# A hybrid layer on one core: two sums moved by one step, a second buffer for a sum of tokens, and the last norm ahead of a split

## The chip, the cores and the metric

The kernel runs on one core of a Trainium2 chip. The core has five engines that run side by side: TensorE (PE in the profile, with its weight loads as PEld), VectorE (DVE), ScalarE (ACT), GpSimd (POOL) and SyncE (SP), which here only issues DMAs. Each engine works through its own list of instructions in order and waits at semaphores for the others. The metric is the device time of one execution in microseconds, lower is better.

## What is computed

One layer of a backbone over 1024 latent tokens and 256 context tokens with 1024 features: a normalised and modulated input goes through one input projection, then an mLSTM head group and a windowed attention head group, an output projection with a residual, and a gated convolutional feed-forward block with a second residual and a last norm. The change lies where attention ends and the feed-forward begins, so these lines matter:

```python
y_a = window_attention(...)
x = x + g_a * (jnp.concatenate([y_m, y_a], axis=-1) @ w_out[l])
x = x + g_f * conv_glu(modulate(rmsnorm(x, norm_ffn[l]), sh_f, sc_f),
                       w_up[l], ffn_conv_w[l], ffn_conv_b[l], w_down[l])

def conv_glu(h, w_up, conv_w, conv_b, w_down):
    a, val = jnp.split(h @ w_up, 2, axis=-1)
    a = jax.nn.gelu(dwconv(a, conv_w, conv_b))
    return (a * val) @ w_down
```

## The kernel before

All products are float32-accurate on a faster format: each operand is split into a high part (a cast, mostly on ScalarE) and a low part (source minus high part, on VectorE), and three matmuls per product are added up. The names end in `h` and `l`. The cast and the subtraction of a split are issued separately, so a split is two places in the code: `split_b(b)` and its kin issue the cast at once and return a function that issues the subtraction.

**Attention** runs over 32 pairs of heads, block by block of 128 tokens, in a software pipeline of steps `t` from 0 to n + 1 with n = 32. In one step different stages serve different pairs: scores of pair t + 1, normalisation of the pair before (`nrm`, GpSimd), transposition to `pt` and split into `ph` and `pl` (L1166, L1172), the product with the values into `u` (L1182), and the two copies and two adds that write `u` into `yT` (L1187 to L1194). There is a single `u` buffer, so the product of one pair waits for the adds of the pair before. Other work is put in at numbered places of a step: `more[t, i]` is a list that `fill(t, i)` issues at place i of step t. Place 3 is ahead of the splits of its step on VectorE. Steps 32 and 33 are the last: there is no new score and few pairs are still in the pipeline.

**The weight sums.** The feed-forward's first matrix is multiplied in a scheme with fewer products than the plain one, in which the operands are sums of quarters: seven operands of tokens (`B11`, `B21`, `B22`, `T1` to `T4`, all in the two tiles `hB`, high and low) and sums of weight quarters. For block 0 of the weights the quarters lie in `ym` during attention, and three operations on VectorE at `more[n, 3]` (step 32) write the sums into `yS`, a view of `yT`. When all readers of `ym` are done, its room is taken by `er`, `e0` and `r1`, into which `load_0` loads quarters again (L1261, issued by SyncE).

**The second residual's input.** After attention a loop goes over the blocks in `order = [4, 1, 5, 2, 6, 3, 7]`. Each takes the output projection of a block (`wout_n`, two halves), adds the residual (L1388), squares it on ScalarE (`sq`), takes the root and its reciprocal (`norm_b`), transposes (`trans`) and moves the result to `raws` (`evac`). From pairs of blocks b - 4 and b, four sums follow: `sum1` to `sum4` on VectorE, and the splits `split_t1` to `split_t4` into `hB`. `sum2` writes to a tile `tb` with one buffer, which `sum4` and `split_t2` read. The projection's input is a split of `yT` into `yh`, `yl` (`ysplit_h`, `ysplit_l`); the first three blocks of the order have buffers of their own, the later four lie in slots of `hB` that are not needed yet.

**The end of that loop.** The last block is 7, `prev` is 3 and `late` is 6. Its norm is the head of a chain: square, root, reciprocal, scaling in two halves (ScalarE and VectorE), transposes, the splits for T1 to T4 of blocks 6 and 7. TensorE meanwhile computes what needs neither (`ps_a`, `ps_a2`), and then the products of block 0: `f` (B22), `c` (T1), `b` (T2), `e` (T3), `d` (T4), and goes on with block 1.

The order of work on TensorE, VectorE, ScalarE and GpSimd is that of the code, written by hand. The order of SyncE's DMAs around the change is chosen by the planner, from L1643 on also by the code.

Of the kernel before, what the change touches and what calls it, by code (L numbers as in the profile page):

```python
# [9 lines left out]
F32 = mybir.dt.float32  # L10
F32R = mybir.dt.float32r
# [7 lines left out]
P = 128  # L19
# [59 lines left out]
def build(tc, I, out, dbg=None):  # L79
    nc = tc.nc  # L80
    dbg = dbg or {}
    V, S, G, T = nc.vector, nc.scalar, nc.gpsimd, nc.tensor
# [41 lines left out]
    ym = rp.tile([P, NL, 512], F32, name="ym")  # L124
# [5 lines left out]
    hl = [hl_(0)]  # L130
# [13 lines left out]
    def load_split(src, w, rawf=None, split=True, alloc=True, now=range(2)):  # L144
        room = lambda: [st.tile([P, KT, XW], F32R, name=n, tag=n)[:].rearrange("p a b -> p (a b)")[:, :KT * w]
                        .rearrange("p (k f) -> p k f", k=KT) for n in ("wh", "wl")]
        hi, lo = room() if alloc else (None, None)
        raws = {}

        def load(q):  # L150
            raws[q] = rawf() if rawf else sr.tile([P, 4, XW], F32, name="wr", tag="wr")
            nc.sync.dma_start(raws[q][:, :, :w], src[:, 4 * q:4 * q + 4, :])

        def cut(q):
            ks, raw = slice(4 * q, 4 * q + 4), raws[q]
            S.copy(hi[:, ks, :w], raw[:, :, :w])
            V.tensor_tensor(out=lo[:, ks, :w], in0=raw[:, :, :w], in1=hi[:, ks, :w].bitcast(F32), op=ALU.subtract)

        if split:
            for q in range(2):  # L160
                load(q)
                cut(q)
            return hi, lo
        for q in now:
            load(q)

        def rest(qs=range(2)):
            nonlocal hi, lo
            if hi is None:
                hi, lo = room()  # L170
            for q in qs:
                cut(q)
            return hi, lo
        rest.load = load
        return rest
# [296 lines left out]
    order = (list(range(NCH)), [1, 0] + list(range(NCH - 1, NC - 1, -1)))  # L472
# [491 lines left out]
    n = 0  # L964
# [12 lines left out]
    for h in range(H):  # L977
# [3 lines left out]
        else:  # L981
            wq = [wkq]
            late = lambda: wq.append(load_split(I["w_q"][1], 256, lambda: pq.tile([P, 4, 256], F32, name="wr", tag="rga")))
# [66 lines left out]
    yslice = lambda b: next(v[:, t.index(b)] for t, v in yTa.items() if b in t)  # L1050
# [3 lines left out]
    t4 = pb_.enter_context(tc.tile_pool(name="t4", bufs=2, reuse_waits="tile"))  # L1054
# [7 lines left out]
    class Wout:  # L1062
# [32 lines left out]
        def add(self, n):  # L1095
            ns = slice(512 * n, 512 * n + 512)
            V.tensor_tensor(out=self.xb[:, ns], in0=self.po[:], in1=self.xb[:, ns], op=ALU.add)
            if n == 1:
                nc.sync.dma_start(x2_d[self.b][:], self.xb[:])
# [96 lines left out]
    order = [4, 1, 5, 2, 6, 3, 7]  # L1196
    ys = {}
    sub = lambda e, o, x, y: e.tensor_tensor(out=o, in0=x, in1=y, op=ALU.subtract)  # L1198

    def ysplit_h(b, eng=G, room=None):  # L1200
        ys[b] = room or [t4.tile([P, 4, P], F32R, name=f"y{n}", tag=f"y{n}", bufs=3)[:] for n in "hl"]
        eng.copy(ys[b][0], yslice(b)) if eng is S else eng.tensor_copy(ys[b][0], yslice(b))

    def ysplit_l(b):
        sub(V, ys[b][1], yslice(b), ys[b][0].bitcast(F32))
# [13 lines left out]
    more = collections.defaultdict(list)  # L1219
# [28 lines left out]
    n = len(pairs)  # L1248
# [4 lines left out]
    more[n - 5, 2] += [lambda: ysplit_l(order[0])]  # L1253
    more[n - 4, 0] += [lambda: ysplit_h(order[1], S)]
    more[n - 3, 0] += [lambda: ysplit_l(order[1])]
    more[n - 2, 0] += [lambda: ysplit_h(order[2], S)]
    add = lambda e, o, x, y: e.tensor_tensor(out=o, in0=x, in1=y, op=ALU.add)
    yS = yTa[2, 0, 4, 1, 5][:].rearrange("p w k t -> p w (k t)")

    def load_0(to, h):  # L1260
        nc.sync.dma_start(to, I["w_up"][0, :, 2 * h:2 * h + 2].rearrange("p q k f -> p q (k f)"))  # L1261

    more[n - 11, 0] += [lambda: load_0(ym[:, 2:4], 0), lambda: load_0(ym[:, 4:6], 1)]
    more[n, 3] += [lambda: add(V, yS[:, 2], ym[:, 5], ym[:, 4]), lambda: sub(V, yS[:, 3], yS[:, 2], ym[:, 2]),
                   lambda: sub(V, yS[:, 1], ym[:, 3], yS[:, 3])]

    attn = tc.manual_schedule(engines={mybir.EngineType.PE, mybir.EngineType.DVE, mybir.EngineType.Activation,
                                       mybir.EngineType.Pool})
# [4 lines left out]
    for t in range(n + 2):  # L1273
# [3 lines left out]
        if t in WOT:  # L1277
            k = 4 + WOT.index(t)
            room = [wop.tile([P, D], F32R, name=f"wo{n}{k}")[:] for n in "hl"]
# [70 lines left out]
    hB = [hbp.tile([P, 7, 4, 512], F32R, name=f"hB{i}") for i in range(2)]  # L1350
    tbk = ExitStack()
    tbp = tbk.enter_context(tc.tile_pool(name="tbp", bufs=1, side="right", reuse_waits="tile"))
    B11, B21, B22, T1, T2, T3, T4 = range(7)
# [19 lines left out]
    hns, rs, pts, raws, tbs = ({} for _ in range(5))  # L1373
    last = order[-1]
# [15 lines left out]
    def mean0(b):  # L1390
        V.tensor_scalar(out=rs[b][:, 2:3], in0=rs[b][:, 0:1], scalar1=1.0 / D, scalar2=EPS, op0=ALU.mult, op1=ALU.add)

    def sq(b, n, mean=True):
        if n == 0:
            hns[b] = t5.tile([P, D], F32, name="hn", tag="hn")
            rs[b] = t5.tile([P, 3], F32, name="r2", tag="r2")
        ns = slice(512 * n, 512 * n + 512)
        S.activation(hns[b][:, ns], xs[b][:, ns], AF.Square, accum_out=rs[b][:, n:n + 1])
        if n == 1:
            if mean:  # L1400
                run(1)
                mean0(b)
            S.activation(rs[b][:, 0:1], rs[b][:, 1:2], AF.Sqrt, bias=rs[b][:, 2:3], scale=1.0 / D)

    def norm_b(b, halves=False):
        run(1)
        V.reciprocal(rs[b][:, 0:1], rs[b][:, 0:1])
        if halves:
            S.activation(hns[b][:, 0:512], xs[b][:, 0:512], AF.Copy, scale=rs[b][:, 0:1])
            V.tensor_scalar(out=hns[b][:, 512:D], in0=xs[b][:, 512:D], scalar1=rs[b][:, 0:1], scalar2=None, op0=ALU.mult)  # L1410
        else:
            S.activation(hns[b][:], xs[b], AF.Copy, scale=rs[b][:, 0:1])
# [28 lines left out]
    def run(n=99):  # L1441
        for _ in range(min(n, len(held))):
            held.pop(0)()

    def split(b, blk, w, src, hi_eng=S):
        ts = slice(b % 4 * P, b % 4 * P + P)
        hi, lo = (hB[i][:, blk:blk + w, :, ts] for i in range(2))
        (S.copy if hi_eng is S else hi_eng.tensor_copy)(hi, src)  # L1448
        return lambda: sub(V, lo, src, hi.bitcast(F32))


    def sum1(b):
        sub(V, raws[b - 4][:, 0], raws[b][:, 0], raws[b - 4][:, 0])

    def sum2(b):
        tbs[b] = tbp.tile([P, 1, 4, P], F32, name="tb", tag="tb", bufs=1)
        sub(V, tbs[b][:, 0], raws[b][:, 1], raws[b - 4][:, 0])

    def sum3(b, e=V):
        sub(e, raws[b][:, 0], raws[b][:, 1], raws[b][:, 0])  # L1460

    def sum4(b, e=V):
        sub(e, raws[b - 4][:, 1], raws[b - 4][:, 1], tbs[b][:, 0])

    split_b = lambda b: split(b, B22, 1, raws[b][:, 1:2])
    split_t1 = lambda b: split(b, T1, 1, raws[b - 4][:, 0:1])
    split_t2 = lambda b: split(b, T2, 1, tbs[b][:])
    split_t3 = lambda b: split(b, T3, 1, raws[b][:, 0:1])
    split_t4 = lambda b: split(b, T4, 1, raws[b - 4][:, 1:2])
# [10 lines left out]
    add = lambda e, o, x, y: e.tensor_tensor(out=o, in0=x, in1=y, op=ALU.add)  # L1480
# [3 lines left out]
    fence.__enter__()  # L1484
    sq(0, 0)
    sq(0, 1)
    for j in range(3, 7):
        ysplit_h(order[j], G, [hB[n][:, B22 + j - 3, :, 3 * P:4 * P] for n in range(2)])
    for j in range(2, 5):
# [3 lines left out]
    late = None  # L1493
    for i, b in enumerate(order):
# [20 lines left out]
        if pp is not None and pp < 4:  # L1515
# [4 lines left out]
            late = None  # L1520
            run(1)
        if pp is not None and pp >= 4:
# [6 lines left out]
            late = pp  # L1529
# [11 lines left out]
    evac(prev)  # L1541
    add1()
    late = pp
    lo_b = split_b(late)
    mean0(last)
    lo3 = split(prev, B11, 2, raws[prev][:], V)
    sq(last, 1, False)
    sum1(late)
    norm_b(last, True)
    lo3()  # L1550
    prod(ps_a, e0, 0, B11, True, True, None, c3)
    prod(ps_a2, e0, 1, B21, True, False, None, c3, range(2))
# [14 lines left out]
    f = ExitStack()  # L1567
# [20 lines left out]
    def wsplit_h(R, n):  # L1588
        src = (R[0] and R[0][:], R[1][:, 2:4], R[1][:, 0:2] if R[0] else r1[:], R[1][:, 4:5] if R[0] else yS[:, 1:2])[n]
        w = src.shape[1]  # L1590
        wt = [fw.tile([P, w, 512], F32R, name=f"w{n}{w}", tag=f"w{n}{w}", bufs=5 if w == 2 else 2) for n in "hl"]
        S.copy(wt[0][:], src)  # L1592

        def lo():
            sub(V, wt[1][:], src, wt[0][:].bitcast(F32))
            return wt
        return lo
# [5 lines left out]
    lo_b = split_b(last)  # L1603
# [9 lines left out]
    lo_2 = split_t2(late)  # L1613
    wS = wS()
    S.copy(ar0[:], ps_a[:])
    lo_1()
    lo_2()
    sum3(late)
    sum4(late)
    sum2(last)  # L1620
    lo_3, lo_4 = split_t3(late), split_t4(late)
    lo_2 = split_t2(last)
    wA = wsplit_h(R, 2)
    lo_2()
    sum3(last)
    lo_5 = split_t3(last)
    lo_3()
# [8 lines left out]
                                                                    tag={"a": "a", "f": "b", "b": "b"}.get(n, "c"))  # L1636
# [118 lines left out]
    for i in range(1, NF):  # L1755
        last = i == NF - 1
# [175 lines left out]
    more = {}  # L1932
# [87 lines left out]
    for t, (p, ps, fresh) in enumerate(products):  # L2020
        for j in range(NP):
            n = NP * t + j
# [34 lines left out]
            if NP + 3 <= n < NP + 3 + NL:  # L2057
                b = n - NP - 3
# [17 lines left out]
    n = len(steps) - 3  # L2076
# [100 lines left out]
```

## Time and profile before

| what | value |
|---|---|
| median of 3 runs | 1268.82 us (1268.67 to 1268.99) |
| profiled execution | 1268.82 us |
| its span | 1267.0 us |
| mean granted TensorE clock | 0.998 |
| instructions in the span | 19250 |

A row of the timeline has: start in us from the span's start, duration in us, engine, line, operation, output and input, shape, how many instructions were merged, and in brackets the engine's idle time before it in us with what ended it. A row of the table by stretches has the stretch, its length, then the busy time and number of instructions of PE, PEld, DVE, ACT and POOL, the granted clock, the busy share of the DMA engines and GB/s. Matmul ends are modelled, so the start of a matmul is firmer than its end.

### The profile page before, as it was taken

The page shows a single profiled execution, that of the slowest core. Times are in us where ns is not written, and L with a number is a line of the kernel's source. Part 1 is how long each engine was busy: PE and PEld are TensorE (multiplying, and loading weights), DVE is VectorE, ACT ScalarE, POOL GpSimd, SP SyncE. Part 2 cuts the span into 40 slices and gives each one's busy share as a digit, 9 for nine tenths or more (in the row PEclk, how much of TensorE's full clock was granted, in tenths as well). Part 3 has the DMA queues.
Part 4 walks back from the last instruction along what each step waited for, and adds up shares of the span by engine and source line. Part 5 has one row for each costly group of instructions (what it writes and reads, how often), then busy time and mean ns, then how long its engine had stood idle before and what let it go on. Part 6 is the DMA issues. An engine that isn't in the chain of part 4 may idle for free.

```text
span 1267.0 us, 19250 instructions
## 1 busy us (share of the span) xinstructions
PE 1234.5 (97%) x7047; PEld 1059.8 (84%) x7047; DVE 974.1 (77%) x1691; ACT 639.0 (50%) x1309; POOL 187.7 (15%) x162
## 2 busy tenths in 40 slices
PE   6999999999999999999999999999999999999997
PEld 4799999999898888887877888888888887788886
DVE  5863777777887888788987877777777776877887
ACT  6632556464865777786843333333333334434435
POOL 1200000000001434221002231233231232001000
PEclk9999999999999999999999999999999999999999
DMA  9541535362255333104313332223322237975553
GB/s 360 184 142 35 144 119 152 116 180 70 85 175 162 130 129 105 59 27 167 116 51 125 111 106 100 94 106 117 101 107 100 92 134 267 337 251 187 194 193 133
DMA packets 90560, 176.17 MB, mean 139 GB/s; under 512 B 12954, under 2 KB 29538, under 8 KB 90466
## 3 DMA queue, kind: packets, MB, share of 16 engines
q1 hardware_dynamic: 90178, 174.15, 40.9%
q8 instruction: 56, 0.92, 0.3%
q10 hardware_dynamic: 288, 0.79, 0.2%
q14 instruction: 38, 0.31, 0.1%
HBM read 136.58 MB, written 38.33 MB: 138 GB/s over the span
## 4 chain that ended last, share of the span: by engine, by line
PE 80%; DVE 7%; ACT 5%; DMA 4%; issue 2%; SPq 1%; POOL 1%; ACTq 0%; DVEq 0%; POOLq 0%
PE pd L2014 14%; PE pa L1476 8%; PE pc L1476 8%; PE pp L588 7%; PE pe L1476 4%; PE pd L1476 4%; PE pb L1476 4%; PE u L1182 3%; PE pv L307 2%; PE pv L309 2%; PE pv L308 2%; PE pt L1159 2%; PE po L307 1%; PE px L309 1%; PE po L309 1%
## 5 line engine op out<-in xcount | busy, mean ns | idle before, releaser
L1592 ACT CAST wh<-Rb 128x1024 fp32r<-128x1024 f32 (+1 forms) x63 | 57.0, 906 | 144.3 <-PE pd L1476 77.2
L2014 PE MATMUL pd<-dh,al 128*128 128x512 f32 x296 | 115.4, 390 | 1.2 <-DVE al L1357 1.2
L2014 PE MATMUL pd<-dh,ah 128*128 128x512 f32 x296 | 115.3, 389 | 0.0
L2014 PE MATMUL pd<-dl,ah 128*128 128x512 f32 x296 | 115.3, 389 | 0.0
L1476 PE MATMUL pc<-hB,wh 128*128 128x512 f32 x344 | 105.6, 389 | 0.0
L1476 PE MATMUL pa<-hB,wh 128*128 128x512 f32 x336 | 103.7, 390 | 0.3 <-ACT sn L1673 0.2
L1198 DVE TENSOR_TENSOR wl<-Rb,wh 128x1024 fp32r<-128x1024 f32 (+1 forms) x63 | 65.8, 1046 | 39.3 <-ACT wh L1592 38.7
L1709 POOL TENSOR_TENSOR tt<-vt,tt 128x512 f32<-128x512 f32 x22 | 29.5, 1342 | 369.0 <-ACT tt L1703 369.0
L588 PE MATMUL pp<-hl,wh 128*128 128x512 f32 x256 | 79.3, 405 | 0.0
L307 PE MATMUL pv<-wh,hl 128*128 128x256 f32 x256 | 75.9, 296 | 0.0
L1476 PEld LDWEIGHTS pc<-hB,wh 128*128 128x128 f32 x344 | 64.6, 188 | 13.5
L1476 PEld LDWEIGHTS pa<-hB,wh 128*128 128x128 f32 x336 | 62.9, 188 | 14.2 <-ACT sn L1673 1.1
L309 PE MATMUL pv<-wh,hl 128*128 128x256 f32 x256 | 72.4, 283 | 0.0
L308 PE MATMUL pv<-wl,hl 128*128 128x256 f32 x256 | 72.3, 282 | 0.0
L2014 PEld LDWEIGHTS pd<-dh,al 128*128 128x128 f32 x296 | 55.6, 188 | 13.2 <-DVE al L1357 1.9
L1476 PE MATMUL pc<-hB,wl 128*128 128x512 f32 x172 | 66.4, 389 | 0.0
L2014 PEld LDWEIGHTS pd<-dl,ah 128*128 128x128 f32 x296 | 55.6, 188 | 11.9 <-DVE dl L1357 0.3
L2014 PEld LDWEIGHTS pd<-dh,ah 128*128 128x128 f32 x296 | 55.6, 188 | 11.8 <-ACT ah L1356 0.3
L1476 PE MATMUL pa<-hB,wl 128*128 128x512 f32 x168 | 65.4, 389 | 0.0
L1166 ACT CAST ph<-pt 128x512 fp32r<-128x512 f32 (+1 forms) x88 | 46.2, 525 | 26.8 <-PE pt L1159 26.5
L1476 PE MATMUL pb<-hB,wh 128*128 128x512 f32 x176 | 54.0, 390 | 0.6 <-ACT hB L1448 0.6
L1136 DVE TENSOR_REDUCE nm<-sps 128x1 f32<-128x641 f32 (+1 forms) x64 | 50.3, 786 | 4.9 <-PE sps L1132 3.4
(1080 smaller groups left out, 3698.9 us busy)
## 6 DMA issues: line engine op xcount, KB each, us to landing
w<-in_w_ada_dram SPq DMA_DIRECT2D x64, 256.0 KB, 2.7
br<-in_w_down_dram SPq DMA_DIRECT2D x25, 512.0 KB, 5.6
ar<-act_s SPq DMA_DIRECT2D x44, 256.0 KB, 3.5
Ra<-in_w_up_dram SPq DMA_DIRECT2D x21, 512.0 KB, 3.6
Rb<-in_w_up_dram SPq DMA_DIRECT2D x21, 512.0 KB, 3.6
act_a<-tt SPq DMA_DIRECT2D x33, 256.0 KB, 2.0
act_s<-tt SPq DMA_DIRECT2D x33, 256.0 KB, 2.0
wr<-in_w_h_dram SPq DMA_DIRECT2D x16, 512.0 KB, 4.0
```

The costliest lines, as they stand in the source:

```text
L307: T.matmul(ps, st_hi, mv_hi, start=first, stop=False)
L308: T.matmul(ps, st_hi, mv_lo, start=False, stop=False)
L309: T.matmul(ps, st_lo, mv_hi, start=False, stop=last)
L588: T.matmul(pp[:, 512 * n:512 * n + 512], wkq[sw][:, kt, cs], hl[n][part][:, kt, :], start=kt == 0 and sw + part == 0, stop=kt == KT - 1 an ...
L1136: V.tensor_reduce(out=self.nm[:, j:j + 1], in_=self.sv[j], axis=AX.X, op=ALU.max, negate=True)
L1166: S.copy(self.ph[i][:, :w], self.pt[i][:, :w])
L1182: T.matmul(self.u[:], vv[:, c, self.g], part[i][:, kk * 2 * P:(kk + 1) * 2 * P], start=kb + m == 0, stop=kb == last and m == 1)
L1198: sub = lambda e, o, x, y: e.tensor_tensor(out=o, in0=x, in1=y, op=ALU.subtract)
L1476: T.matmul(ps[:, cols], wt[sw][:, j, kt * P:kt * P + P], hB[part][:, blk, kt, cols], start=first and n == 0, stop=last and n == len(seq) - ...
L1592: S.copy(wt[0][:], src)
L1709: G.tensor_tensor(out=self.tt[:, h2_], in0=self.vt[:], in1=self.tt[:, h2_], op=ALU.mult)
L2014: T.matmul(ps[:], ac[sa][:, js], w[sw], start=first and n == 0, stop=last and n == 2, skip_group_check=not fresh)
```

## The change

Three parts, which a fourth makes room for.

First, of the three sums of block 0's weights only the first stays in step 32; the second and third go to the same place of step 33. Second, after the loop, the split of block 6 for B22 (`lo_b = split_b(late)`, whose cast is on ScalarE) is issued behind the norm of block 7 instead of ahead of its square. Third, `tb` has two buffers, and `sum2(last)` with the split for T2 goes ahead of `sum3(late)` and `sum4(late)`. For the room, `yl` has two buffers instead of three, and the low part of the third block of the order (block 5) lies in the slot of `hB` that T4 of block 7 takes later.

```diff
     def ysplit_h(b, eng=G, room=None):
-        ys[b] = room or [t4.tile([P, 4, P], F32R, name=f"y{n}", tag=f"y{n}", bufs=3)[:] for n in "hl"]
+        room = room or [None, None]
+        ys[b] = [a if a is not None else t4.tile([P, 4, P], F32R, name=f"y{n}", tag=f"y{n}", bufs=3 if n == "h" else 2)[:]
+                 for a, n in zip(room, "hl")]
...
-    more[n - 2, 0] += [lambda: ysplit_h(order[2], S)]
+    yh2 = []
+    more[n - 2, 0] += [lambda: yh2.append(t4.tile([P, 4, P], F32R, name="yh", tag="yh", bufs=3)[:]),
+                       lambda: S.copy(yh2[0], yslice(order[2]))]
...
-    more[n, 3] += [lambda: add(V, yS[:, 2], ym[:, 5], ym[:, 4]), lambda: sub(V, yS[:, 3], yS[:, 2], ym[:, 2]),
-                   lambda: sub(V, yS[:, 1], ym[:, 3], yS[:, 3])]
+    more[n, 3] += [lambda: add(V, yS[:, 2], ym[:, 5], ym[:, 4])]
+    more[n + 1, 3] += [lambda: sub(V, yS[:, 3], yS[:, 2], ym[:, 2]), lambda: sub(V, yS[:, 1], ym[:, 3], yS[:, 3])]
...
-        tbs[b] = tbp.tile([P, 1, 4, P], F32, name="tb", tag="tb", bufs=1)
+        tbs[b] = tbp.tile([P, 1, 4, P], F32, name="tb", tag="tb", bufs=2)
...
+    ys[order[2]] = [yh2[0], hB[1][:, T4, :, 3 * P:4 * P]]
     for j in range(3, 7):
...
     late = pp
-    lo_b = split_b(late)
     mean0(last)
     lo3 = split(prev, B11, 2, raws[prev][:], V)
     sq(last, 1, False)
     sum1(late)
     norm_b(last, True)
+    lo_b = split_b(late)
     lo3()
...
     lo_1()
+    sum2(last)
     lo_2()
+    lo_2 = split_t2(last)
     sum3(late)
-    sum4(late)
-    sum2(last)
-    lo_3, lo_4 = split_t3(late), split_t4(late)
-    lo_2 = split_t2(last)
+    lo_3 = split_t3(late)
     wA = wsplit_h(R, 2)
     lo_2()
+    sum4(late)
+    lo_4 = split_t4(late)
     sum3(last)
```

## The prediction

> **What bounds the kernel now.** I read the page's busy table first, then the busy time by stretches, then TensorE's timeline with the idle time before each row.
>
> ```profile
> PE 1234.5 (97%) x7047; PEld 1059.8 (84%) x7047; DVE 974.1 (77%) x1691; ACT 639.0 (50%) x1309; POOL 187.7 (15%) x162
> ```
> ```profile
> 585.00:622.00 37.00, 37.00 (x188) 31.07 (x187) 35.03 (x76) 28.87 (x66) 0.00 (x0) 1.00 0.53 185
> ...
> 700.00:1000.00 300.00, 300.00 (x1325) 248.40 (x1324) 231.16 (x256) 102.87 (x112) 75.92 (x48) 1.00 0.30 105
> ```
> ```profile
> 572.66 0.47 PE L1182 MATMUL u<-ph,vv 128*128 128x256 f32 x2 [1.58 <-DVE yT L1194]
> ...
> 627.11 0.65 PE L1424 MATMUL pt<-ident,hn 128*128 128x128 f32 x4 [0.49 <-DVE hn L1410]
> ...
> 638.05 1.20 PE L1476 MATMUL pb<-hB,wh 128*128 128x512 f32 x4 [0.63 <-ACT hB L1448]
> ...
> 650.07 0.50 PE L1476 MATMUL pb<-hB,wl 128*128 128x512 f32 x1 [0.30 <-DVE wl L1198]
> ```
>
> The first row says TensorE is the resource: 1234.5 of 1267.0 us. The stretches (TensorE is the second figure) say it never rests from 585 to 622 or from 700 to 1000. So an edit to VectorE or ScalarE pays only if it shortens one of TensorE's few pauses, and what it wins there lasts, because behind the pause TensorE alone sets the pace. The four timeline rows are the pauses beside the change: one per part of it, and the last just downstream. Together they hold 3.0 us; no more can be won than about that and the slow restart after each.
>
> **Part A: two of block 0's sums go from step 32 to step 33.**
>
> ```profile
> 568.53 0.67 DVE L1257 TENSOR_TENSOR yT<-ym 128x512 f32<-128x512 f32 x1
> 569.24 1.07 DVE L1198 TENSOR_TENSOR yT<-yT,ym 128x512 f32<-128x512 f32 x1
> 570.34 1.07 DVE L1198 TENSOR_TENSOR yT<-ym,yT 128x512 f32<-128x512 f32 x1
> 571.33 0.68 DVE L1172 TENSOR_TENSOR pl__7377<-pt,ph 128x512 fp32r<-128x512 f32 x1
> 571.93 0.27 DVE L1193 TENSOR_TENSOR yT<-u,ut 64x128 f32<-64x128 f32 x1
> 572.22 0.29 DVE L1194 TENSOR_TENSOR yT<-u,ut 64x128 f32<-64x128 f32 x1
> ...
> 575.48 0.69 DVE L1172 TENSOR_TENSOR pl__7416<-pt,ph 128x512 fp32r<-128x512 f32 x1 [1.65 <-ACT ph L1166]
> ...
> 583.72 0.68 DVE L1510 CAST e0h<-er 128x1024 fp32r<-128x1024 f32 x1
> ```
> ```profile
> 569.28 0.59 ACT L1166 CAST ph<-pt 128x512 fp32r<-128x512 f32 x1 [0.86 <-PE pt L1159]
> ...
> 574.86 0.59 ACT L1166 CAST ph<-pt 128x512 fp32r<-128x512 f32 x1 [3.81 <-PE pt L1159]
> ```
> ```profile
> 570.68 0.40 PE L309 MATMUL po<-woh,yml 128*128 128x512 f32 x1
> ...
> 578.12 0.40 PE L1182 MATMUL u<-pl__7416,vv 128*128 128x256 f32 x2
> ```
>
> The three sums hold VectorE until 571.41. Behind them wait the split `pl__7377` and the two adds of L1193 and L1194, and these empty the one `u` buffer that TensorE wants at 572.66. Take the last two sums away: the split's other input is ScalarE's `ph`, done at 569.28 + 0.59 = 569.87, so it starts at 569.90 (0.03 for the hand-over, as from 574.86 + 0.59 to 575.48). The adds end 572.51 - 571.33 = 1.18 after the split's start, so at 571.08, and TensorE follows 0.15 later as now (572.66 - 572.51), at 571.23, with its own earlier work done at 571.08. The start moves by 572.66 - 571.23 = **1.43 us**. What is late next is the same chain, by 0.15 us.
>
> The sums now stand ahead of the split `pl__7416` on VectorE. There it idled 1.65 us for ScalarE; two sums at 0.69 take 1.4, at today's 1.07 they take 2.2 and push the split by 0.5. Its reader is the `u` matmul at 578.12, 1.95 after the split's end (576.17), so I cost them at nothing either way; without that slack they would cost up to 0.5. Why were they 1.07 long?
>
> ```profile
> 554.36 0.70 POOL L1147 TENSOR_SCALAR p__7138<-p__7138,ss 128x512 f32<-128x512 f32 x1
> ...
> 568.78 0.99 POOL L1147 TENSOR_SCALAR p__7322<-p__7322,ss 128x512 f32<-128x512 f32 x1 [3.14 <-DVE ss L1144]
> ```
> ```profile
> 554.45 0.69 DVE L1172 TENSOR_TENSOR pl__7182<-pt,ph 128x512 fp32r<-128x512 f32 x1 [0.36 <-ACT ph L1166]
> ```
>
> GpSimd ran beside them and was itself slow (0.99 against 0.70). The split `pl__7182` ran beside GpSimd at its plain 0.69, so I leave the advanced split at 0.69. The lower bound, had it 1.07, is 1.43 - 0.39 = 1.04 us. [...]
>
> The two loads into `er` and `r` are issued when the old `ym` is free, so they move with the last sum.
>
> ```profile
> 571.49 0.33 SPq L1261 DMA_DIRECT2D er<-in_w_up_dram  x1
> ...
> 584.30 0.33 SPq L1378 DMA_DIRECT2D x<-x_d  x1
> ```
> ```profile
> er<-in_w_up_dram SPq DMA_DIRECT2D x1, 512.0 KB, 4.0
> ```
>
> The sums end near 573.8, the load lands at 573.8 + 0.1 + 4.0 = 577.9, and the first reader is the cast of L1510 at 583.72 - 1.43 = 582.3: 4.4 us of cover. The low part of block 5's `y` in a free slot of `hB` has the same operation, type and length as in its old buffer: nothing.
>
> **Part B: the norm of block 7 ahead of a split on ScalarE.**
>
> ```profile
> 624.73 0.65 ACT L1448 CAST hB<-raw 128x512 fp32r<-128x512 f32 x1
> 625.25 0.67 ACT L1398 ACTIVATE hn<-x 128x512 f32<-128x512 f32 x1
> ...
> 626.04 0.29 ACT L1403 ACTIVATE r<-r 128x1 f32<-128x1 f32 x1
> ```
> ```profile
> 624.09 0.69 DVE L1388 TENSOR_TENSOR x<-po,x 128x512 f32<-128x512 f32 x1
> ...
> 625.52 0.68 DVE L1198 TENSOR_TENSOR raw<-raw 128x512 f32<-128x512 f32 x1
> 626.37 0.16 DVE L1407 RECIPROCAL r<-r 128x1 f32<-128x1 f32 x1 [0.17 <-ACT r L1403]
> 626.57 0.49 DVE L1410 TENSOR_SCALAR hn<-x,r 128x512 f32<-128x512 f32 x1
> ```
>
> Without the cast in front, the square starts when its input is added, 624.09 + 0.69 + 0.03 = 624.81 instead of 625.25: 0.44 earlier, the root then ends at 625.89. But the reciprocal stands behind the sum of 625.52 on VectorE, and unhindered operations of this kind start 0.60 apart (571.33 to 571.93). So it starts at 626.12, not 626.37: the gain is **0.25**, not 0.44, and VectorE's sum is late next. TensorE still pauses about 0.24 there. The cast now runs behind ScalarE's half of the norm, until about 627.6, still ahead of its reader. Bounds: 0.1, if the casts behind it slip, to 0.44.
>
> **Part C: the sum for T2 ahead of sums 3 and 4, with a second `tb` buffer.**
>
> ```profile
> 635.92 0.69 DVE L1198 TENSOR_TENSOR raw<-raw,tb 128x512 f32<-128x512 f32 x1
> 636.65 0.69 DVE L1198 TENSOR_TENSOR tb<-er,raw 128x512 f32<-128x512 f32 x1
> 638.03 0.69 DVE L1198 TENSOR_TENSOR hB<-tb,hB 128x512 fp32r<-128x512 f32 x1 [0.69 <-ACT hB L1448]
> ```
> ```profile
> 637.38 0.62 ACT L1448 CAST hB<-tb 128x512 fp32r<-128x512 f32 x1
> ```
> ```profile
> 635.45 1.07 PE L1476 MATMUL pc<-hB,wl 128*128 128x512 f32 x4
> 636.36 1.07 PE L1476 MATMUL pc<-hB,wh 128*128 128x512 f32 x4
> ...
> 639.08 1.08 PE L1476 MATMUL pb<-hB,wl 128*128 128x512 f32 x4
> ```
>
> Groups of four matmuls start 0.91 apart, so `pb` could start at 637.27 and its second group at 638.18; they start at 638.05 and 639.08. The stall costs 0.90. Moved up three places, the sum ends about 635.4 and its cast about 636.1: over a us early, and the whole 0.90 goes. On VectorE the order saves too: 636.65 is 0.13 later than the usual 0.60 (it waits for the reader of the single `tb`), 638.03 is 0.78 late; 0.91 in all. So the later splits for T3 and T4 arrive 0.91 earlier while TensorE asks for them 0.90 earlier, and stay covered.
>
> Downstream, the pause at 650.07 is for a low part of block 1's weights, VectorE's own chain. TensorE arrives there 0.25 + 0.90 = 1.15 earlier, the weights 0.25 + 0.91 = 1.16 earlier: the pause stays and the smaller counts, **1.15** for B and C together. [...]
>
> **The sum.** 1.43 + 1.15 = 2.58. The profiled execution took 1268.82 (span 1267.0, and 1.82 around it), equal to the median of the runs. 1268.82 - 2.58 = **1266.24**. With part A at 1.04 and B at 0.1 it is 1266.8; with B at 0.44 and the pause of 650.07 halved, 1265.9. A measurement of this kernel can tell about 0.2%, that is 2.54 us: the forecast lies on that line.
>
> **Rivals.** *T2's stall becomes a stall for T4*: the last split is only just in time, and if ScalarE's new order delays it, C gives back its 0.90: 1267.14. For it: a ScalarE that serves five casts and a weight split there; against: the 0.91 that VectorE gains. *Step 32 stays late*: something else holds `u` (another add on VectorE, ScalarE's copies): only 1.15, so 1267.67. Against: ScalarE's `ph` is the only other input. *Nothing arrives*: the gains are taken back at a later wait on a load; 1268.8. Against: no rest from 700 to 1000. *Slower*: SyncE's order isn't written out here. If the load of `x` (584.30, waiting for block 0's norm) is put ahead of the now later `er` load, that lands near 582.9 + 0.4 + 4.0 = 587.3, 5.0 after 582.3 where VectorE wants it. VectorE has 37.00 - 35.03 = 2.0 of rest up to 622, so 3.0 would stay against the 2.58 won: 1269.2. It decides from a landing at 582.3 + 2.0 + 2.6 = 586.9 on; before that it only eats the gain. Against it: `er` is first in line today, 12.8 us ahead of that load.
>
> **How the numbers follow.** The forecast 0.75, of it 0.42 beyond the line; T4 0.11; step 32 0.06; nothing 0.03; slower 0.05, mostly within the line. Faster 0.42, same 0.55, slower 0.03. The range takes the forecast's bounds and the T4 case and leaves out the rest: 1265.7 to 1267.5.
>
> **What would show it.** A: TensorE's pause before the `u` matmul of step 32 near 0.15, both sums near 0.69 in step 33. B: the square right behind the add, the reciprocal right behind the sum. C: no pause before `pb`; 650.07's pause as now, at 647.5. Wrong, if a pause of over 0.3 us appears at T3, T4 or the cast into `e0`, or a new order on SyncE.

## The result and the profile after

| | before | after |
|---|---|---|
| median of 13 runs each, us | 1269.17 (1267.98 to 1271.46) | 1266.61 (1265.63 to 1268.54) |
| profiled execution, us | 1268.82 | 1265.89 |
| its span, us | 1267.0 | 1264.1 |
| mean granted TensorE clock | 0.998 | 0.998 |

The ratio after to before is 0.9978, with an interval of 0.9971 to 0.9986: 2.8 us less, and between 1.8 and 3.7; the medians differ by 2.56. The forecast was 2.58 us less, 1266.24. Line numbers of the changed kernel are four higher than before from about L1257 on, and six higher at its end.

First TensorE's timeline of the changed kernel at the same places as in the prediction, with one earlier row as a common mark, 562.16. The same row of the kernel before follows in a second fence.

```profile
562.16 0.48 PE L1182 MATMUL u<-ph,vv 128*128 128x256 f32 x2 [0.56 <-ACT p__7264 L1140]
...
570.84 0.40 PE L309 MATMUL po<-woh,yml 128*128 128x512 f32 x1
571.38 0.47 PE L1182 MATMUL u<-ph,vv 128*128 128x256 f32 x2
...
572.62 0.50 PE L1182 MATMUL u<-pl__7392,vv 128*128 128x256 f32 x2 [0.30 <-DVE pl__7392 L1172]
...
625.54 0.66 PE L1428 MATMUL pt<-ident,hn 128*128 128x128 f32 x4 [0.18 <-DVE hn L1414]
...
635.70 1.07 PE L1480 MATMUL pb<-hB,wh 128*128 128x512 f32 x4
636.61 1.07 PE L1480 MATMUL pb<-hB,wl 128*128 128x512 f32 x4
...
641.14 1.17 PE L1480 MATMUL pd<-hB,wh 128*128 128x512 f32 x4
...
647.58 0.50 PE L1480 MATMUL pb<-hB,wl 128*128 128x512 f32 x1 [0.29 <-DVE wl L1198]
```
```profile
562.01 0.47 PE L1182 MATMUL u<-ph,vv 128*128 128x256 f32 x2 [0.55 <-ACT p__7264 L1140]
```

The pause of 1.58 us ahead of `u` and the one of 0.63 ahead of `pb` have no bracket any more; the one at the transposes shrank from 0.49 to 0.18; the one for block 1's weights is as long as it was. Measured between starts, from the mark on, the path splits so (each figure is the difference of two rows' starts, here or in the prediction; the last residual add on VectorE starts at 624.09 before and 622.83 after):

| stretch of the path, us | before | after | difference |
|---|---|---|---|
| mark to `u` of step 32 | 10.65 | 9.22 | -1.43 |
| `u` to the last residual add | 51.43 | 51.45 | +0.02 |
| that add to the transposes | 3.02 | 2.71 | -0.31 |
| transposes to second group of `pb` | 11.97 | 11.07 | -0.90 |
| that group to the weights' pause | 10.99 | 10.97 | -0.02 |
| sum | 88.06 | 85.42 | -2.64 |

So 2.64 of the 2.9 us between the two spans came from the three places that the change touches. The mark itself came 0.15 later, and 0.42 was won far behind: from the weights' pause to the row at 1070.85 it is 420.78 us before, and to the same row after (1067.94) 420.36. Most of this is one pause at a place that the change does not touch, for a low part of the down projection, 0.53 us before and 0.25 after. When the same changed kernel was profiled again (below) that pause was 0.53, so it is not counted as the change's.

VectorE in steps 32 and 33, from its timeline after the change:

```profile
568.68 0.67 DVE L1261 TENSOR_TENSOR yT<-ym 128x512 f32<-128x512 f32 x1
570.04 0.69 DVE L1172 TENSOR_TENSOR pl__7374<-pt,ph 128x512 fp32r<-128x512 f32 x1 [0.69 <-ACT ph L1166]
570.65 0.27 DVE L1193 TENSOR_TENSOR yT<-u,ut 64x128 f32<-64x128 f32 x1
570.94 0.29 DVE L1194 TENSOR_TENSOR yT<-u,ut 64x128 f32<-64x128 f32 x1
...
572.48 0.68 DVE L1198 TENSOR_TENSOR yT<-yT,ym 128x512 f32<-128x512 f32 x1
573.20 0.69 DVE L1198 TENSOR_TENSOR yT<-ym,yT 128x512 f32<-128x512 f32 x1
574.22 0.69 DVE L1172 TENSOR_TENSOR pl__7415<-pt,ph 128x512 fp32r<-128x512 f32 x1 [0.33 <-ACT ph L1166]
```

The split `pl__7374` now waits for ScalarE's `ph` and for nothing on its own engine. The two sums take 0.68 and 0.69 instead of 1.07, and of the 1.65 us of rest ahead of the next split 0.33 is left, so they are still free. SyncE's timeline shows what the prediction named as the way to a slower kernel:

```profile
573.96 0.33 SPq L1265 DMA_DIRECT2D er<-in_w_up_dram  x1
...
583.02 0.33 SPq L1382 DMA_DIRECT2D x<-x_d  x1
```

The load into `er` is issued behind the last sum, and the load of `x` stays behind it.

The norm of block 7, VectorE and then ScalarE:

```profile
622.83 0.69 DVE L1392 TENSOR_TENSOR x<-po,x 128x512 f32<-128x512 f32 x1
...
624.21 0.69 DVE L1198 TENSOR_TENSOR raw<-raw 128x512 f32<-128x512 f32 x1
624.81 0.16 DVE L1411 RECIPROCAL r<-r 128x1 f32<-128x1 f32 x1
625.00 0.48 DVE L1414 TENSOR_SCALAR hn<-x,r 128x512 f32<-128x512 f32 x1
```
```profile
623.56 0.64 ACT L1402 ACTIVATE hn<-x 128x512 f32<-128x512 f32 x1
...
624.31 0.30 ACT L1407 ACTIVATE r<-r 128x1 f32<-128x1 f32 x1
...
625.63 0.60 ACT L1452 CAST hB<-raw 128x512 fp32r<-128x512 f32 x1
```

The square follows the add (622.83 + 0.69 = 623.52, and 623.56), the cast stands behind the norm, and the reciprocal has no bracket: it starts 0.60 behind the sum, held by its own engine and no longer by ScalarE.

The sum for T2 and its two users, VectorE and ScalarE:

```profile
633.16 0.68 DVE L1198 TENSOR_TENSOR tb<-er,raw 128x512 f32<-128x512 f32 x1
```
```profile
633.88 0.62 ACT L1452 CAST hB<-tb 128x512 fp32r<-128x512 f32 x1 [0.66 <-DVE tb L1198]
...
640.43 0.62 ACT L1452 CAST hB<-raw 128x512 fp32r<-128x512 f32 x1 [2.74 <-DVE raw L1198]
```

The cast for T2 ends at 634.50, 1.2 us before `pb` (635.70). The cast for T4 ends at 641.05, and TensorE goes on at 641.14: the rival, that T2's stall becomes one for T4, stayed away by 0.09 us.

### The profile page after: what moved, and what is told of

Its sections match the earlier page's. It is cut to its first block, busy times and chain, and to the rows that moved or that the text cites. A ratio compares the mean times of both kernels' runs of the same rounds, so it can differ in the third digit from the quotient of the medians.

```text
span 1264.1 us, 19253 instructions
## 1 busy us (share of the span) xinstructions
PE 1234.4 (98%) x7047; PEld 1060.2 (84%) x7047; DVE 972.8 (77%) x1691; ACT 637.9 (50%) x1309; POOL 187.1 (15%) x162
## 4 chain that ended last, share of the span: by engine, by line
PE 84%; DVE 6%; ACT 5%; DMA 3%; issue 2%; POOL 1%; SPq 0%; ACTq 0%; DVEq 0%; POOLq 0%
PE pd L2020 14%; PE pa L1480 8%; PE pc L1480 8%; PE pp L588 7%; PE pe L1480 4%; PE pd L1480 4%; PE pb L1480 4%; PE u L1182 3%; PE pv L307 2%; PE pv L309 2%; PE pv L308 2%; PE po L307 2%; PE po L309 2%; PE po L308 2%; PE pt L1159 2%
## 5 line engine op out<-in xcount | busy, mean ns | idle before, releaser
L1480 PE MATMUL pd<-hB,wh 128*128 128x512 f32 x176 | 54.0, 390 | 0.0
```

The costliest lines, as they stand in the source:

```text
L1480: T.matmul(ps[:, cols], wt[sw][:, j, kt * P:kt * P + P], hB[part][:, blk, kt, cols], start=first and n == 0, stop=last and n == len(seq) - ...
```

## The experiments

Eleven runs, in three groups that each shared the runs of the kernel before: medians 1269.62 (31 runs) for the first four, 1269.47 (28) for the next four, 1269.76 (22) for the last three.

### Each part alone

The theory: three parts that add up, 1.43, about 0.25 and 0.90.

**The sums alone**, on the kernel before:

```diff
-    more[n, 3] += [lambda: add(V, yS[:, 2], ym[:, 5], ym[:, 4]), lambda: sub(V, yS[:, 3], yS[:, 2], ym[:, 2]),
-                   lambda: sub(V, yS[:, 1], ym[:, 3], yS[:, 3])]
+    more[n, 3] += [lambda: add(V, yS[:, 2], ym[:, 5], ym[:, 4])]
+    more[n + 1, 3] += [lambda: sub(V, yS[:, 3], yS[:, 2], ym[:, 2]), lambda: sub(V, yS[:, 1], ym[:, 3], yS[:, 3])]
```

> Part A alone. Theory (TensorE alone sets the pace behind each pause, so the parts add up): the u matmul of step 32 starts 1.4 us earlier than in the kernel before, its pause falls from 1.58 to about 0.15, both moved sums take about 0.69, and everything behind is 1.4 earlier, with the pauses before the transposes (0.49) and before pb (0.63) as they were; time about 1.4 us less. Rival (VectorE, hardly idle from 585 to 622, holds the rest): the 1.4 shrinks on the way, the pause before the transposes grows, and less than 0.7 is left at the end.

Measured: 1267.68, ratio 0.9984 (0.9975 to 0.9993), so 2.0 us less (0.9 to 3.2). From the mark to the weights' pause 86.57 us, 1.49 less than before, of which the first stretch has 1.44 (563.59 to 572.80, 9.21). The pauses downstream are those of before: 0.43 at the transposes, 0.68 at `pb`. Part A gives its 1.43 by itself. That the medians differ by a little more has a reason of its own, to which the last group leads.

**The norm alone**: `lo_b = split_b(late)` behind `norm_b(last, True)`, all else as before.

> Part B alone. Theory: reciprocal right behind the sum, transposes 0.25 to 0.3 earlier; VectorE's chain to T2 is earlier by the same, so the pause before pb stays 0.63 and the 0.25 to 0.3 arrives at the end. Rival (T2's chain sets the end there without part C): the pause before pb grows to about 0.9 and nothing is left.

Measured: 1269.21, ratio 0.9999 (0.9989 to 1.0008). Two or three tenths of a microsecond can't be told apart by medians here. The trace has them: add to transposes 2.90 us (627.45 to 630.35) against 3.02, so 0.12 where 0.25 to 0.3 had been expected. One profile isn't enough for a term this small, as the table further below shows. This profile also held something that none of the theories had, a half granted clock, once at about 30 us and once shortly behind the pause of step 32; more on it at the end.

**T2's order and buffer alone**: A and B of the change undone.

> Part C with its room, without A and B. Theory: no pause before pb, its second group 0.9 earlier; T3 and T4 covered; the pause for block 1's weights stays at 0.3; time 0.9 us less. Rival (the stall moves to T4): a pause of 0.5 or more before pd, and at most 0.4 us less.

Measured: 1269.28, ratio 0.9989 (0.998 to 0.9999). Between medians that is 0.3 us, by the ratio 1.4, and the interval reaches from 0.1 to 2.5. The trace is sharper: the transposes to the second group of `pb` take 11.06 us (627.37 to 638.43) against 11.97, no pause ahead of `pb`, and mark to weights 87.09, 0.97 less. The term is 0.9, as predicted.

**The second buffer alone**: the order of before, `bufs=2` for `tb`, with the room that it needs made as in the change (only the line of `tb` is shown).

```diff
-        tbs[b] = tbp.tile([P, 1, 4, P], F32, name="tb", tag="tb", bufs=1)
+        tbs[b] = tbp.tile([P, 1, 4, P], F32, name="tb", tag="tb", bufs=2)
```

> The second tb buffer with its room alone, all work in the old order. Theory (the wait for the reader of the single buffer costs 0.13): the sum for T2 starts 0.60 instead of 0.73 after the one in front, its cast and pb come 0.13 earlier and the pause before pb is 0.50. [...]

Measured: 1269.74, ratio 1.0002 (0.9992 to 1.0012); no difference by time. From this kernel's timeline, VectorE and TensorE:

```profile
636.65 0.68 DVE L1198 TENSOR_TENSOR raw<-raw,tb 128x512 f32<-128x512 f32 x1
637.25 0.68 DVE L1198 TENSOR_TENSOR tb<-er,raw 128x512 f32<-128x512 f32 x1
```
```profile
638.63 1.21 PE L1480 MATMUL pb<-hB,wh 128*128 128x512 f32 x4 [0.50 <-ACT hB L1452]
```

The sum into `tb` starts 0.60 behind the operation ahead of it, where it was 0.73 with a single buffer, and TensorE's pause is 0.50 instead of 0.63; the second group of `pb` comes 11.86 us behind the transposes against 11.97. The wait for the buffer was worth the 0.13 that the row of before suggested, or 0.11 by the second group; the rest of the 0.90, nearly 0.8, is the order.

### Is it the place or GpSimd?

In step 32 of the kernel before the two sums took 1.07 each, from 569.24 to 571.41, and GpSimd was at work from 568.78 to 570.87, with two operations of 0.99 and 1.12. A rival for part A was that it is the slow sums that cost, so that any place without GpSimd would do. **The two sums later in the same step**, at `more[n, 0]`:

```diff
-    more[n, 3] += [lambda: add(V, yS[:, 2], ym[:, 5], ym[:, 4]), lambda: sub(V, yS[:, 3], yS[:, 2], ym[:, 2]),
-                   lambda: sub(V, yS[:, 1], ym[:, 3], yS[:, 3])]
+    more[n, 3] += [lambda: add(V, yS[:, 2], ym[:, 5], ym[:, 4])]
+    more[n, 0] += [lambda: sub(V, yS[:, 3], yS[:, 2], ym[:, 2]), lambda: sub(V, yS[:, 1], ym[:, 3], yS[:, 3])]
```

> Kernel before, with the second and third sum still in step 32 but behind the adds that empty u (place 0 instead of 3). Theory (it is the place in VectorE's order that costs): the u matmul starts 1.4 earlier, but the split of the second transposes now waits behind both sums, its matmul pauses about 1.5 us, and at most 0.2 us of the 1.4 is left. Rival (it is the slow sums beside GpSimd that cost): the sums take 0.69 each and 0.7 us is left.

Measured: 1269.75, ratio 1.0001 (0.9992 to 1.0011). TensorE's timeline of this kernel:

```profile
571.71 0.48 PE L1182 MATMUL u<-ph,vv 128*128 128x256 f32 x2
...
574.38 0.79 PE L1182 MATMUL u<-pl__7395,vv 128*128 128x256 f32 x2 [1.72 <-DVE pl__7395 L1172]
```

The sums ran at 0.69 here, from 571.59 to 573.01, with GpSimd idle (busy 0.00 us from 571 to 574), and the kernel gained nothing. The first `u` matmul came 9.23 behind the mark, as early as with part A, but the pause only went on to the last `u` group of the step, which waits for the split `pl__7395` behind the sums. Mark to this matmul is 11.90 (from 562.48) against 11.88 before (573.89 - 562.01). So it is the place that pays: step 33 has 1.65 us of rest on VectorE, step 32 has none.

### What is late next at the norm, and how near T4 is

The prediction said that B gets 0.25 and not 0.44 because `sum1` stands ahead of the reciprocal on VectorE. **`norm_b(last, True)` ahead of `sum1(late)`**, on the change:

```diff
-    sum1(late)
     norm_b(last, True)
+    sum1(late)
     lo_b = split_b(late)
```

> The change, with sum1 of block 6 behind the norm of block 7 on VectorE too. Theory (the reciprocal's wait for that sum is worth less than the sum's cover): transposes 0.15 earlier than in the change, but VectorE idles about 0.4 there, all its later splits come 0.4 later, and T4 has only 0.1 to spare, so a pause of about 0.3 appears before pd; time 0.1 to 0.3 us more than the change. Rival (only the norm's chain counts): 0.15 us less than the change.

Measured: 1266.84, ratio 0.9981 (0.9972 to 0.999); the change itself in the same group 1266.44. The two timelines, VectorE and TensorE:

```profile
624.67 0.16 DVE L1411 RECIPROCAL r<-r 128x1 f32<-128x1 f32 x1 [0.33 <-ACT r L1407]
```
```profile
641.59 1.20 PE L1480 MATMUL pd<-hB,wh 128*128 128x512 f32 x4 [0.31 <-ACT hB L1452]
```

The reciprocal waits for ScalarE again, the transposes come 2.54 us behind the add (622.87 to 625.41) and have no pause. But the sum that was pushed back pushes the splits, and TensorE stops 0.31 for T4 (`pd`). Mark to weights is 85.87, against 85.42 and 85.59 for the change: a loss of 0.3 to 0.45. Both are shown: that `sum1` was what held the norm, and that T4's cover of 0.09 is used up at once.

### The change again, and two more pauses

**The change once more**, for its scatter:

> The change itself, beside the one before. 2.6 us less than the kernel before, by the pauses; the extra 0.3 that its first profile showed at the loads near 1070 may or may not come back.

Measured: 1266.44, ratio 0.9975 (0.9965 to 0.9984). Mark to weights 85.59 (562.17 to 647.76), the pause at the transposes 0.33 (0.18 in the first profile).

**Two more pauses taken away**, on the change: a residual add behind the split `pl__7392` in step 32, and two sums of block 1's weights ahead of two adds.

```diff
+    add0_f = more[n, 1].pop()
+    more[n, 2] += [add0_f]
...
-    add(V, B.u2[:], ps0["b"][:], ar0[:])
     sums_v(R)
-    add(V, ar0[:], ps_a2[:], ar0[:])
+    add(V, B.u2[:], ps0["b"][:], ar0[:])
     add(V, u2b[:], ps0["f"][:], B.u2[:])
     W[1] = wsplit(R, 1)
+    add(V, ar0[:], ps_a2[:], ar0[:])
```

> The change, with two more moves of its kind: in step 32 the residual's add goes behind the split of the second transposes, and block 1's weight sums go ahead of block 0's first add, with one add behind the weights' split. Theory: the pauses of 0.30 before the u matmul and of 0.29 before pb of block 1 go, each with about 0.1 of restart; 0.8 us less than the change, 3.4 less than before. Rival (the moved add holds po, or pb needs the bank that the add frees): a new pause of the same size at the next matmul into po or pb, and no difference from the change.

Measured: 1266.36, ratio 0.9977 (0.9967 to 0.9987), no difference from the change that can be measured, where 0.8 us less had been expected. Both pauses, 0.30 and 0.29, are gone from the trace, and a new one stands behind them, for the adds that were pushed back:

```profile
660.34 0.70 PE L1482 MATMUL pc<-hB,wh 128*128 128x512 f32 x2 [0.26 <-DVE av L1486]
```

The second move, of the weights' sums, gave back all that it won: from the mark to the pause near 689 us it is 126.67 us with the change, 126.29 with both moves (688.50) and 126.32 with the first move alone (688.87). **The first move without the second**:

> The change with only the first of the two further moves: the residual's add behind the split of the second transposes in step 32. Theory: the pause of 0.30 before the u matmul of that split goes, everything behind is 0.4 to 0.5 earlier than in the change, and no new pause follows: 0.4 to 0.5 us less. Rival (VectorE gives it back, as the second move did behind block 1): a new pause near the transposes of block 7, and no difference.

Measured: 1265.91, ratio 0.9966 (0.9954 to 0.9978), 4.3 us less than before (2.8 to 5.8). TensorE's timeline:

```profile
572.56 0.40 PE L1182 MATMUL u<-pl__7391,vv 128*128 128x256 f32 x2
...
647.64 0.50 PE L1482 MATMUL pb<-hB,wl 128*128 128x512 f32 x1 [0.31 <-DVE wl L1198]
```

No pause at the `u` matmul of the low part any more. Mark to weights is 85.09 (from 562.55), 0.33 less than the first profile of the change and 0.50 less than the second. It has the lowest median of all; its interval overlaps that of the change.

### The pause itself

After the second group a question was open: why do the medians of part A fall by more than 1.43? The executions of the kernel before fall into two lots by their mean granted clock, and the profiles of two kernels that keep the pause in step 32 (the norm alone, the sums later in the step) showed a half clock behind it. If the pause causes that, filling it must bring the clock back without taking any work off the path, and a longer pause must make it worse. **The pause filled**: 13 transposes of the identity that nobody reads, ahead of the first `u` matmul of step 32, on the kernel before.

```diff
+        if t == n:
+            sp_ = pSs[0][0].tile([P, 1024], F32, name="sps", tag=pSs[0][1])
+            for _ in range(13):
+                T.transpose(sp_[:, 0:P], ident[:], ident[:])
         C.pv(0)
```

> Kernel before, with 13 idle transposes on TensorE (0.11 us each, results unused) in the pause of step 32; VectorE's order and the wait are as before. Theory (the pause lets the granted clock fall to half for some 3 us in about a third of the executions, which costs 1.5 us each time, and the change also wins by ending that): no clock below 1.00 between 570 and 585, the mean clock of an execution at 0.997 or less in at most 1 of 10 instead of about 3 of 10, the median 0.2 to 0.6 us below the kernel before, although the wait is the same. Rival (the clock falls by itself): as many executions with a lower clock as before, and the same median.

**The pause made longer**: the first sum of step 32 two more times, which writes the same values again.

```diff
+    more[n, 3] += [lambda: add(V, yS[:, 2], ym[:, 5], ym[:, 4])] * 2
```

> Kernel before, with the first of the three sums done three times in step 32, so that the pause before the u matmul becomes about 3.2 us. Theory (a longer pause lets the clock fall more often): a lower clock right behind the pause in most executions, and the time 2.2 to 3.2 us above the kernel before, of which 1.4 to 1.8 is the wait itself. Rival (the clock falls by itself): 1.4 to 1.8 us above, with as many low clocks as before.

Measured: filled, 1269.41, ratio 0.9996 (0.9987 to 1.0005); longer, 1272.09, ratio 1.0019 (1.001 to 1.0028). Their timelines, first the filled one:

```profile
571.82 1.58 PE L1329 MATMUL sps<-ident 128*128 128x128 f32 x13
573.57 0.47 PE L1182 MATMUL u<-ph,vv 128*128 128x256 f32 x2 [0.17 <-DVE yT L1194]
```
```profile
574.61 0.48 PE L1182 MATMUL u<-ph,vv 128*128 128x256 f32 x2 [3.05 <-DVE yT L1194]
```

By the median the filled kernel can't be told from the one before. By the clock, 1 of its 11 executions had a mean granted clock of 0.997 or less, against 8 of 22 of the kernel before in the same group and 7 of 11 with the longer pause. These counts lean the way of the theory, but they are too small to settle it alone.

The longer pause costs more than itself: 1.46 us at the wait (568.79 to 574.61, 5.82, against 4.36), 2.3 in the median. This fits the number that the theory of the clock had expected, but not its reason: the profile shows no clock below 1.00 behind the pause. It shows 53.02 us between `u` and the last residual add (574.61 to 627.63) against 51.43, at full clock, and a pause of TensorE for VectorE's `x`:

```profile
616.20 0.50 PE L307 MATMUL po<-woh,hB 128*128 128x512 f32 x1 [0.44 <-DVE x L1389]
```

The two additional sums push back all of VectorE's later work, and between 585 and 622 it has only 2.0 us of rest (37.00 - 35.03). So in this profile the cost beyond the wait comes without a lower clock, and it fits VectorE's lateness. The executions say the same: among those with a mean clock above 0.997 the longer pause costs 2.7 us (medians of 1271.86 against 1269.12). That a longer pause costs more by the clock is not shown here.

## Why the prediction was right

**What bounds the kernel.** TensorE's busy time stayed (1234.5 before) and the pauses got shorter:

```profile
PE 1234.4 (98%) x7047; PEld 1060.2 (84%) x7047; DVE 972.8 (77%) x1691; ACT 637.9 (50%) x1309; POOL 187.1 (15%) x162
```

The rule that what is won at a pause lasts held: 51.43 and 51.45 us between `u` and the last add, 10.99 and 10.97 behind `pb`. The one exception was 0.3 us that came and went at a late pause between two profiles of the same kernel.

**Part A, 1.43.** Measured 1.43 and, alone, 1.44. The split stayed at 0.69 (570.04) beside an operation of GpSimd (569.89 to 570.58), so the lower bound (1.04) didn't come about. The sums in step 33 cost nothing and ran in 0.68 and 0.69, the better of the two cases named. What is late next is the same chain by some 0.15: TensorE's own work ended at 570.84 + 0.40 = 571.24 and it went on at 571.38.

**Part B, 0.25.** Its mechanism was right (the row 624.81, and the experiment that put `sum1` behind the norm), and so was its size, though single profiles seem to say otherwise: 0.31 in one, 0.16 in the other. The scatter has a cause in the trace. Two operations ahead of the reciprocal VectorE does a cast whose input ScalarE copies (`raw`). In the first profile of the change this cast doesn't wait, in the second it does:

```profile
623.60 0.69 DVE L1452 CAST hB<-raw 128x1024 fp32r<-128x1024 f32 x1
```
```profile
623.76 0.69 DVE L1452 CAST hB<-raw 128x1024 fp32r<-128x1024 f32 x1 [0.17 <-ACT raw L1439]
```

Sorted by this wait, which is 0.17 to 0.23 us where there is one, the time from add to transposes in all profiles is:

| order at the norm | the cast waits | profiles, us | mean |
|---|---|---|---|
| split ahead of the square | no (5 profiles) | 3.02, 2.95, 2.96, 2.96, 3.01 | 2.98 |
| split ahead of the square | yes (2) | 3.17, 3.17 | 3.17 |
| norm ahead, `sum1` ahead of the reciprocal | no (2) | 2.71, 2.73 | 2.72 |
| norm ahead, `sum1` ahead of the reciprocal | yes (3) | 2.90, 2.86, 2.92 | 2.89 |
| norm ahead of `sum1` too | no (1) | 2.54 | 2.54 |

Like compared with like, the gain is 0.26 and 0.28. Without the wait, moving `sum1` too gives 0.44 (2.98 - 2.54), which is the upper bound that the prediction set. Why ScalarE's copy ends later in some profiles stays open.

**Part C, 0.90.** Measured 0.90 with the change and 0.91 alone, 0.11 to 0.13 of it from the buffer. The prediction read 0.13 for the wait for the single `tb` from the row 636.65, and with the buffer alone the start moved from 0.73 to 0.60 behind the operation ahead, and the pause from 0.63 to 0.50. The changed kernel has a distance of that size too: its sum at 573.20, which reads what the sum at 572.48 wrote, starts 0.72 behind it, and that one 0.60 behind the split at 571.88, which it doesn't read.

**Downstream.** The pause for block 1's weights stayed, 0.29 for 0.30, at 647.58 where 647.5 had been forecast.

**The sum.** 1.43 + 0.26 + 0.90 is 2.59, the path from mark to weights gave 2.64 in one profile and 2.47 in the other, and the medians 2.56. The forecast of 1266.24 was 0.37 below the measured median mainly because the kernel before had a median of 1269.17 over 13 runs and not the 1268.82 of its first three. That the medians agree with the forecast's 2.58 to 0.02 is luck: in the group in which the change ran once more they differ by 3.03 (1269.47 - 1266.44). The forecast has no term for the clock of the kernel before, which the last section is about. It had 0.42 for a gain beyond 0.2% and 0.55 for one short of it; 0.22% was measured, and the interval (0.14% to 0.29%) leaves open on which side it lies.

**The rivals.** A stall for T4 didn't come, by 0.09 us, and came in the experiment that delayed the splits; its chance was not too high. Step 32 came out on time. SyncE kept its order, and `er` was issued at 573.96, within 0.2 us of the forecast.

## What to carry to other kernels

Where one engine is busy for 97% of the time, an edit on another engine is worth the length of the pause that it shortens, up to the next operation that is late there (1.43, 0.26 and 0.90 us here, and 2.64 less by the path), and that can be read from the trace to a tenth of a microsecond: find the pause, the operation that ends it, and what stands ahead of that on its engine. Moving an operation pays only into rest that the trace shows, as the sums that moved within their step showed, and a cover of 0.1 us is enough until the next edit. Where medians differ by more than the path explains, look at the granted clock of each execution, and in the profile at where it is low, before inventing a mechanism.

## What the runs showed of the hardware

**At a pause of 1.6 or 1.7 us TensorE's clock was a half for about 3.4 us in two of six profiles.** The pause in step 32 of the kernel with the norm alone, and windows of 1 us behind it (TensorE's busy time is the second figure, the granted clock the third from the end):

```profile
574.15 0.47 PE L1182 MATMUL u<-ph,vv 128*128 128x256 f32 x2 [1.60 <-DVE yT L1194]
```
```profile
572.00:573.00 1.00, 0.55 (x3) 0.12 (x1) 1.00 (x2) 0.53 (x1) 0.36 (x1) 1.00 0.00 0
573.00:574.00 1.00, 0.00 (x0) 0.00 (x0) 0.99 (x3) 0.00 (x0) 0.00 (x0) 1.00 0.29 29
...
575.00:576.00 1.00, 0.72 (x4) 0.62 (x4) 0.32 (x1) 0.00 (x0) 0.00 (x0) 0.79 0.83 258
576.00:577.00 1.00, 1.00 (x6) 1.00 (x5) 0.00 (x0) 0.10 (x1) 0.00 (x0) 0.50 1.02 410
...
578.00:579.00 1.00, 1.00 (x6) 1.00 (x5) 0.70 (x3) 0.04 (x1) 0.00 (x0) 0.50 0.00 0
579.00:580.00 1.00, 1.00 (x6) 0.84 (x5) 0.34 (x1) 0.58 (x1) 0.00 (x0) 1.00 0.08 16
```

The clock is at a half from about 575.6 to 579, beginning 1.4 us behind the end of the pause. In the other profile that caught it (the sums later in the step) it begins at about 574.2, just ahead of the pause's end, and ends at about 577.6 (means of 0.60, 0.50, 0.50 and 0.69 in the windows of 1 us from 574 to 578), and from the matmul at 574.38 to the transposes it took 54.70 us against 53.22 before (573.89 to 627.11): 1.5 us more for the same work. The four other profiles with the pause unfilled show no half clock there, the one with 3.05 us among them, and neither do the six without a long pause and the filled one.

The same half clock also comes elsewhere. The profiles of the norm alone and of the buffer alone have it at about 30 us, where no kernel differs from the one before; the longest pause that their rows show in the 10 us ahead of it is 0.60. From the buffer alone:

```profile
30.00:32.00 2.00, 2.00 (x11) 2.00 (x11) 2.00 (x4) 2.00 (x4) 2.00 (x3) 0.50 1.04 391
```

It lasts about 3.4 us there too (an estimate from this kernel's means of 0.98, 0.50 and 0.67 in the windows of 2 us from 28 to 34). So it does not come behind a long pause alone, and the mean clock of an execution doesn't say where it was low: this profiled execution has a mean of 0.997 from the place at 30 us alone. What the mean can show is a difference between kernels. Counting the executions with a mean granted clock of 0.997 or less over all groups in which the clock of each run of both kernels is known, and the first group of the change:

| kernels | such executions |
|---|---|
| kernel before (pause 1.6 us) | 25 of 81 |
| the norm alone, T2 alone, the buffer alone, the sums later in the step (pause 1.6 or 1.7) | 19 of 40 |
| pause made longer (3.05) | 7 of 11 |
| pause filled | 1 of 11 |
| no long pause in step 32 (the change twice, the sums alone, `sum1` behind, two more, the add behind the split) | 2 of 56 |

In the kernel before they are 1.1 to 1.8 us longer (medians of 1270.99 against 1269.17, 1270.31 against 1269.25, 1270.61 against 1269.12 in the three groups). With the pause in step 32 they are 44 of 121, without it 2 of 56, and the sums alone make this difference (0 of 10, against 11 of 31 in the same group). By these counts this is what part A won beyond its 1.43. Among executions above 0.997 the sums alone gained 1267.68 - 1269.17 = -1.49, as the trace has it, and over all of them 1267.68 - 1269.62 = -1.94. With the longer pause the two lots differ by only 0.5 us; why was not found. The filled pause points the same way, but weakly: at the share of the kernel before, 25 of 81, one or none of 11 executions would come out in about one such group of ten (an estimate from these counts). That the pause itself, and not the order of work around it, lowers the clock is likely and not proven.

What sets the half clock off was not shown: it came at pauses of 1.6 and 1.7 us in two profiles and at none in four others with pauses from 1.57 to 3.05, and at 30 us it came with none above 0.60 ahead of it. How much work in the pause would be enough to keep the full clock was not measured.

**A float32 product took longer than a matmul of a split.** In the profile of the kernel before, a product of 129 columns on float32 tiles (L733) is two matmuls, and the next product starts 0.22 us behind it (320.38 to 320.60). Of the matmuls of a split with 256 columns just ahead of it, one starts 0.12 behind the other (320.14 to 320.26).
